# A feed-forward opening in a hybrid encoder layer: even and odd activations in shared buffers, a first product over one pair of token tiles, and an operand built inside the first unit

## The chip, the cores and the metric

The kernel runs on one core of a Trainium2 chip. The metric is the device time of one execution, in microseconds (us). Most of a kernel's time is its span, from the first to the last instruction. The engines are TensorE (PE, with its weight loads shown apart as PEld), VectorE (DVE), ScalarE (ACT), GpSimd (POOL) and SyncE (SP, which here issues nearly all DMAs). Instructions on one engine run in the order in which the program lists them; engines wait for each other by semaphores.

## The reference

One layer works on x of 1024 tokens by 1024 features, all in float32:

```
x = x + 1/2 * SwiGLU_1(RMSNorm(x))          # FFN 1
x = x + W_out [attention || HGRN2 both ways]  # mixer, one shared input projection
x = x + 1/2 * SwiGLU_2(RMSNorm(x))          # FFN 2
x = RMSNorm(x)

SwiGLU(h) = (silu(h @ w_gate) * (h @ w_up)) @ w_out      # hidden width 2816
```

The change lies in the first half of each SwiGLU, silu(h @ w_gate) * (h @ w_up). The mixer between the two is the same before and after.

## The kernel before

**Number format.** A float32 product is made of three passes in a faster format: each operand is split into a high part (a rounding cast on ACT, L103 or L185) and a low part (operand minus high part, a subtraction on DVE or POOL, L104 or L186). PE adds high x high, high x low and low x high into one PSUM bank. So each matmul of the algorithm is three instructions, and each operand must be cast and subtracted before use.

**Up projection (ffn_up).** The 1024 tokens lie in 8 tiles of 128. Four pairs (an even and an odd tile each, function pair, for FFN 1 pair1) are loaded; in FFN 1 each tile is normalised first: a square with sum on ACT (L121), nine small steps on DVE for 1/sqrt (rstd, L82 to L94), a scaling on DVE (L131). FFN 2 reads tiles that attention has already normalised and written to memory.

The activations form a 2 x 2 block matrix: B11 and B21 are the lower and upper 512 features of the even tiles, B12 and B22 those of the odd tiles. Function blocks(i) puts pair i into columns i*128 to i*128+127 of these four, each by h_op: four PE transposes into a PSUM bank (L182), a cast on ACT (L185), a subtraction on DVE (L186). The weights of one block f of 128 hidden columns form another 2 x 2: A11, A12 (gate, lower and upper features) and A21, A22 (up). There are 22 such blocks.

Blocks f = 0 and 1 are done plainly (function plain, L277: 8 block products; 96 matmuls of 256 columns for each half g of the columns). The other 20 are done by unit(f) with a scheme of seven block products in place of eight (L294, 12 matmuls of 512 columns each): A11 B11 and A12 B21, then S2 T2, A22 T4, S3 T3, S1 T1 and S4 B22. S1 to S4 are sums of weight blocks (made on POOL, L254 to L257), T1 to T4 sums of activation blocks, made by sums(i): t1 and t2 on DVE (L220, L222), t3 and t4 on POOL (L221, L223), and T2, T4 and T3 by h_op. T1 is put off: t1 is written to memory (L224), and last_sum reads it back (L230) and builds T1 when the buffer of B12, which only the plain blocks read, is free.

Each result goes through silu (ACT) and a product (DVE) and is written to act[f] in memory. Down projection and the rest follow later.

**Order of the opening.** blocks(0) and blocks(1); plain products of f = 0 and 1 over columns 0:256; sums and blocks of the others; plain products over 256:512; sums of pairs 2 and 3; last_sum four times; then the units, interleaved two by two:

```
for i in range(2):
    tiles[i] = blocks(i)
for f in range(early):
    A[f] = [weight_op(f, f"A{i}", src, early_lo) ...]
    plain(f, 0, A[f])
for i in range(2):
    sums(i, *tiles[i])
    tiles[i + 2] = blocks(i + 2)
for f in range(early):
    plain(f, 1, A[f])
```

This is the order of the program; a planner with a timeline of its own then fixes the order on each engine. Where several instructions are ready, the one that stands earlier in the program goes first.

**Buffers.** Pools hand out slots and make a new user wait until the old one has been read: B 4 slots (B11, B21, B12, B22, then T1 for B12), T 3, raw 7 (token tiles and raw weights), wop 9 (split weights, and the junk output of the squares), s 4 (t1 to t4, s1 to s4 and the reloaded t1), n 3 (snapshots p1, u2, u3 of PSUM), c 4 (results), PSUM 8 banks. The argument early_lo names the engine of the low parts of the plain blocks' weights: POOL in FFN 1, DVE in FFN 2.

Of the kernel before, what the change touches and what calls it, by code (L numbers as in the profile page):

```python
# [12 lines left out]
F32 = mybir.dt.float32  # L13
F32R = mybir.dt.float32r
# [3 lines left out]
ALU = mybir.AluOpType  # L18
# [3 lines left out]
P = 128  # L22
# [22 lines left out]
class Trunk:  # L45
# [142 lines left out]
    def ffn_up(self, name, pair, act, early_lo, mid):  # L188
# [75 lines left out]
        def result(what, nm):  # L264
            return self.cc.tile([P, 512], F32, name=f"{what}_{name}_{nm}", tag="c")

        def plain(f, g, A):

            cols = slice(g * 256, (g + 1) * 256)
            ps = [self.bank(f"pp{j}_{name}_{f}_{g}") for j in range(2)]  # L270
            for odd in ((0, 1) if g == 0 else (1, 0)):
                B = [op(key) for key in (("B12", "B22") if odd else ("B11", "B21"))]
                for j in range(2):
                    for k in range(NK):
                        ks = slice((k % 4) * P, (k % 4 + 1) * P)
                        for i, (a, b) in enumerate(((0, 0), (0, 1), (1, 0))):
                            nc.tensor.matmul(  # L277
                                ps[j][:, odd * 256 : (odd + 1) * 256],
                                A[2 * j + k // 4][:, a, ks], B[k // 4][:, b, k % 4, cols],
                                start=(k == 0 and i == 0), stop=(k == NK - 1 and i == 2),  # L280
                            )
            sg = result("sg", f"{f}_{g}")
            nc.scalar.activation(sg, ps[0], AF.Silu)
            nc.vector.tensor_mul(sg, sg, ps[1])
            nc.sync.dma_start(
                act[f].rearrange("p (h t) -> p h t", h=2)[:, :, cols],
                sg.rearrange("p (h t) -> p h t", h=2),
            )

        def product(ps, A, key, first):  # L290
            for k in range(4):
                ks = slice(k * P, (k + 1) * P)
                for i, (a, b) in enumerate(((0, 0), (0, 1), (1, 0))):
                    nc.tensor.matmul(  # L294
                        ps, A[:, a, ks], T[key][:, b, k, :],
# [4 lines left out]
        def unit(f):  # L300
# [43 lines left out]
        tiles = {}  # L344
        for i in range(2):
            tiles[i] = blocks(i)
        A = {}
        for f in range(early):
            A[f] = [weight_op(f, f"A{i}", src, early_lo) for i, src in enumerate(raw_weights(f))]
            plain(f, 0, A[f])  # L350
        for i in range(2):
            sums(i, *tiles[i])
            tiles[i + 2] = blocks(i + 2)
        for f in range(early):
# [623 lines left out]
def trunk_kernel(tc, io):  # L978
    nc = tc.nc
    with ExitStack() as ctx:  # L980
# [12 lines left out]
        def ffn(ctx, name, xn_pair, load, done, d_spec, opened, early_lo, mid=None, finish=None):  # L993
# [6 lines left out]
            with ExitStack() as up:  # L1000
                k.B, k.T = sbuf(up, "B", 4, side="right"), sbuf(up, "T", 3, side="right")
# [15 lines left out]
        with ExitStack() as c1:  # L1017
            gain = []

            def pair1(i):  # L1020
# [7 lines left out]
                for xt, t in zip(x, (2 * i, 2 * i + 1)):  # L1028
                    junk = k.wop.tile([P, D], F32R, name=f"junk_{t}", tag="wop").bitcast(F32)
                    k.norm_rows(xt, gain[0], xt, f"n0_{t}", junk=junk)  # L1030
# [125 lines left out]
```

## Time and profile before

| | us |
|---|---|
| three runs, median (lowest to highest) | 2119.46 (2116.44 to 2119.88) |
| the profiled execution | 2116.49 |
| its span | 2114.7 |
| FFN 1: first plain matmul, first matmul of the units | 29.97, 98.25 |
| FFN 2: first plain matmul, first matmul of the units | 1407.79, 1480.50 |

The profile is of one execution. A row of the timeline gives the start and length of one or more like instructions, the engine, the line of the code and the tiles; brackets hold the idle time before it and what ended it. A row of the windows gives, for one stretch of the span, how long each engine was busy. A busy PE is not always at its pace: waiting between pipelined matmuls is partly counted as busy, and the granted clock (PEclk, 1.00 is full) may be lower.

### The profile page before, as it was taken

How to read it: one execution, taken by the hardware profiler on the slowest of the kernel's cores; microseconds unless marked ns; L12 is line 12 of the kernel's file. 1: busy time of each engine (PE TensorE's matmuls, PEld its weight loads, DVE VectorE, ACT ScalarE, POOL GpSimd, SP SyncE). 2: the span in 40 equal slices, each digit the busy share in tenths (PEclk: the TensorE clock that was granted, in tenths of full speed). 3: DMA queues.
4: the chain of work that ended last, by engine and by line, in shares of the span. 5: the costliest groups of instructions: out<-in, count | busy, mean ns of one | idle time of the engine just before them, and what ended most of it. 6: DMA issues, size and time to landing. Idle time of an engine off the chain costs nothing.

```text
span 2114.7 us, 27958 instructions
## 1 busy us (share of the span) xinstructions
PE 2032.2 (96%) x10849; PEld 1754.3 (83%) x10849; DVE 1166.2 (55%) x1951; ACT 780.3 (37%) x1295; POOL 392.5 (19%) x278
## 2 busy tenths in 40 slices
PE   5899999999999899999999999988999999999998
PEld 5888888887888798989999788878888888878886
DVE  6565555545363506788872567753655555443634
ACT  4333333334343313333332546632433333333432
POOL 2333222310000000121120423311423222100000
PEclk9999999999999999999999999999999999999999
DMA  5422332127464211121234532263322221264542
GB/s 168 119 86 80 94 92 76 56 82 258 148 228 141 80 41 40 31 80 35 86 96 141 172 111 80 84 220 106 100 84 72 84 90 55 75 244 147 180 146 80
DMA packets 208124, 232.12 MB, mean 110 GB/s; under 512 B 9444, under 2 KB 169464, under 8 KB 207992
## 3 DMA queue, kind: packets, MB, share of 16 engines
q1 hardware_dynamic: 205688, 221.95, 33.3%
q0 software_dynamic: 2304, 8.39, 1.0%
q8 instruction: 85, 1.39, 0.3%
q14 instruction: 47, 0.39, 0.1%
HBM read 175.78 MB, written 54.53 MB: 109 GB/s over the span
## 4 chain that ended last, share of the span: by engine, by line
PE 90%; DVE 5%; DMA 2%; issue 1%; ACT 1%; POOL 0%; SPq 0%; DVEq 0%; ACTq 0%; POOLq 0%
PE py_ffn L402 22%; PE pa_ffn L294 15%; PE pd_ffn L294 10%; PE rec_ps L167 6%; PE pc_ffn L294 5%; PE pb_ffn L294 5%; PE pp_ffn L277 5%; PE ri_ps L495 2%; PE rg_ps L495 2%; PE py L855 2%; PE lv L561 2%; PE s L798 2%; PE pv L830 2%; PE pa L855 1%; PE aq_ps L495 1%
## 5 line engine op out<-in xcount | busy, mean ns | idle before, releaser
L402 PE MATMUL py_ffn<-hl_out_ffn,hl_act_ffn 128*128 128x512 f32 x2112 | 481.0, 390 | 4.5 <-ACT hl_out_ffn L103 3.4
L402 PEld LDWEIGHTS py_ffn<-hl_out_ffn,hl_act_ffn 128*128 128x128 f32 x2112 | 396.3, 188 | 88.4 <-ACT hl_out_ffn L103 4.9
L104 DVE TENSOR_TENSOR hl_out_ffn<-raw_out_ffn,hl_out_ffn 128x512 fp32r<-128x512 f32 x176 | 120.3, 689 | 233.9 <-ACT hl_out_ffn L103 233.8
L294 PE MATMUL pa_ffn<-ffn_T,hl_in_ffn_S 128*128 128x512 f32 x960 | 236.8, 390 | 0.0
L294 PEld LDWEIGHTS pa_ffn<-ffn_T,hl_in_ffn_S 128*128 128x128 f32 x960 | 180.4, 188 | 37.2
L103 ACT CAST hl_out_ffn<-raw_out_ffn 128x512 fp32r<-128x512 f32 x176 | 107.6, 619 | 265.1 <-PE py_ffn L402 248.6
L104 DVE TENSOR_TENSOR hl_in_ffn_S<-s_ffn,hl_in_ffn_S 128x512 fp32r<-128x512 f32 x160 | 167.3, 1050 | 25.4 <-ACT hl_in_ffn_S L103 22.0
L103 ACT CAST hl_in_ffn_S<-s_ffn 128x512 fp32r<-128x512 f32 x160 | 99.1, 621 | 192.0 <-PE pd_ffn L294 148.1
L104 DVE TENSOR_TENSOR hl_in_ffn_A<-raw_in_ffn,hl_in_ffn_A 128x512 fp32r<-128x512 f32 x128 | 106.7, 838 | 113.0 <-ACT hl_in_ffn_A L103 113.0
L103 ACT CAST hl_in_ffn_A<-raw_in_ffn 128x512 fp32r<-128x512 f32 x136 | 83.8, 624 | 174.9 <-PE pc_ffn L294 75.3
L167 PE MATMUL rec_ps<-hm,hl_rec_w 128*128 128x512 f32 x576 | 135.9, 395 | 0.0
L167 PEld LDWEIGHTS rec_ps<-hm,hl_rec_w 128*128 128x128 f32 x576 | 108.1, 190 | 21.8
L294 PE MATMUL pd_ffn<-ffn_T,hl_in_ffn_S 128*128 128x512 f32 x480 | 121.8, 389 | 0.0
L294 PE MATMUL pb_ffn<-ffn_B,hl_in_ffn_A 128*128 128x512 f32 x480 | 121.5, 390 | 0.0
L294 PE MATMUL pa_ffn<-ffn_B,hl_in_ffn_A 128*128 128x512 f32 x480 | 116.0, 391 | 0.0
L294 PE MATMUL pc_ffn<-ffn_T,hl_in_ffn_A 128*128 128x512 f32 x480 | 115.3, 390 | 0.0
L294 PE MATMUL pd_ffn<-ffn_B,hl_in_ffn_S 128*128 128x512 f32 x456 | 109.5, 390 | 0.0
L277 PE MATMUL pp_ffn<-ffn_B,hl_in_ffn_A 128*128 128x256 f32 x768 | 100.2, 293 | 6.6 <-ACT xn_n L121 2.2
L294 PEld LDWEIGHTS pa_ffn<-ffn_B,hl_in_ffn_A 128*128 128x128 f32 x480 | 90.4, 189 | 18.5
L294 PEld LDWEIGHTS pb_ffn<-ffn_B,hl_in_ffn_A 128*128 128x128 f32 x480 | 90.2, 188 | 18.6
L294 PEld LDWEIGHTS pc_ffn<-ffn_T,hl_in_ffn_A 128*128 128x128 f32 x480 | 90.2, 188 | 18.6
L294 PEld LDWEIGHTS pd_ffn<-ffn_T,hl_in_ffn_S 128*128 128x128 f32 x480 | 90.2, 188 | 18.6
(245 smaller groups left out, 3127.2 us busy)
## 6 DMA issues: line engine op xcount, KB each, us to landing
raw_in_ffn<-in_ffn_w_in SPq DMA_DIRECT2D x88, 512.0 KB, 4.1
raw_out_ffn<-in_ffn_w_out SPq DMA_DIRECT2D x88, 512.0 KB, 3.8
raw_act_ffn<-d_act SPq DMA_DIRECT2D x88, 256.0 KB, 4.0
d_act<-g_ffn SPq DMA_DIRECT2D x80, 256.0 KB, 2.2
x<-d_x SPq DMA_DIRECT2D x24, 512.0 KB, 4.9
x<-in_x SPq DMA_DIRECT2D x16, 512.0 KB, 5.1
d_x<-x SPq DMA_DIRECT2D x16, 512.0 KB, 2.8
raw_rec_w<-in_w_in_mix SPq DMA_DIRECT2D x12, 512.0 KB, 3.8
```

The source lines that it names most:

```text
L103: nc.scalar.copy(hl[:, 0, :], src)
L104: (lo_engine or nc.vector).tensor_sub(hl[:, 1, :], src, hl[:, 0, :].bitcast(F32))
L167: nc.tensor.matmul(out, hl[:, a, ks], h[half][b][:, k, cols], start=(k == 0 and i == 0), stop=(k == NK - 1 and i == 2),)
L277: nc.tensor.matmul(ps[j][:, odd * 256 : (odd + 1) * 256], A[2 * j + k // 4][:, a, ks], B[k // 4][:, b, k % 4, cols], start=(k == 0 and i = ...
L294: nc.tensor.matmul(ps, A[:, a, ks], T[key][:, b, k, :], start=(first and k == 0 and i == 0), stop=(k == 3 and i == 2), skip_group_check=True,)
L402: nc.tensor.matmul(py[d], ah[:, a, o : o + P], wo[d][:, b, :], start=(f == 0 and i == 0), stop=(f == NF - 1 and i == 2),)
L495: nc.tensor.matmul(ps[:, tt, :], h[half][a][:, k, ts], hl[k // 4][:, b, ws], start=(k == 0 and i == 0), stop=(k == NK - 1 and i == 2),)
L561: nc.tensor.matmul(pl[:, cs], now[:, 0, cs], now[:, 1, cs], start=True, stop=True)
L798: nc.tensor.matmul(ps[:, ks], qT[:, a, qs], kT[:, b, kv, ks], start=(i == 0), stop=(i == 2))
L830: nc.tensor.matmul(ps, vt[:, j, a, vs], pT[j][:, b, i4, :], start=(st == 0 and i == 0), stop=(st == NT - 1 and i == 2),)
L855: nc.tensor.matmul(py, lhs(a, n), units[n][:, b, ds], start=(n == 0 and i == 0), stop=(n == 3 and i == 2),)
```

## The change

Three things change, for both FFNs unless said otherwise.

1. B11 and B12 lie in one buffer, B21 and B22 in another (function both). plain takes a range of columns and reads even and odd tiles with one matmul, so its moving operand has two runs. T1 is written over B12 in place.
2. The order of the opening: block 0 over columns 0:128 after pair 0 alone; then pair 1 and block 1 over 0:256; then pairs 2 and 3 with the sums; then block 0 over 128:256 and 256:512 and block 1 over 256:512. t1 is loaded back, in the n and c pools, after the last sums, and T1 is built inside the first unit, behind its second product.
3. In FFN 1 the low parts of the plain weights are made on DVE; the squares share one junk buffer; the 1/sqrt of pairs 1 to 3 is done jointly for the two tiles (twelve steps on two columns), that of pair 0 tile by tile.

```diff
         def op(key):
+            if key[0] == "B" or key == "T1":
+                row, col = ("1", 1) if key == "T1" else (key[1], int(key[2]) - 1)
+                return both(row)[:, col]
             if key not in T:
-                pool = self.T if key in ("T2", "T3", "T4") else self.B
-                T[key] = pool.tile([P, 2, 4, 512], F32R, name=f"{name}_{key}", tag="T")
+                T[key] = self.T.tile([P, 2, 4, 512], F32R, name=f"{name}_{key}", tag="T")
+            return T[key]
+        def both(row):
+            key = f"B{row}"
+            if key not in T:
+                T[key] = self.B.tile([P, 2, 2, 4, 512], F32R, name=f"{name}_{key}", tag="B")
             return T[key]
...
-        def last_sum(i):
-            t1 = self.sums.tile([P, 512], F32, name=f"t1b_{name}_{i}", tag="s")
+        def load_sum(i):
+            pool, tag = (self.snap, "n") if i < 3 else (self.cc, "c")
+            t1 = pool.tile([P, 512], F32, name=f"t1b_{name}_{i}", tag=tag)
             nc.sync.dma_start(t1, t1s[i * P : (i + 1) * P, :])
-            self.h_op(op("T1"), t1, i, f"{name}_T1")
+            return t1
...
-        def plain(f, g, A):
-            cols = slice(g * 256, (g + 1) * 256)
+        def plain(f, A, lo, hi):
+            w = hi - lo
+            ps = [self.bank(f"pp{j}_{name}_{f}_{lo}") for j in range(2)]
+            halves = lambda t: t[:, : 2 * w].rearrange("p (h t) -> p h t", h=2)
+            B = [both(row) for row in "12"]
+            for j in range(2):
+                for k in range(NK):
+                    ks = slice((k % 4) * P, (k % 4 + 1) * P)
+                    for i, (a, b) in enumerate(((0, 0), (0, 1), (1, 0))):
+                        nc.tensor.matmul(
+                            halves(ps[j]), A[2 * j + k // 4][:, a, ks],
+                            B[k // 4][:, :, b, k % 4, lo:hi],
+                            start=(k == 0 and i == 0), stop=(k == NK - 1 and i == 2),
+                        )
...
             a = bank("pa")
             product(a, A["A11"], "B11", True)
-            p1 = snap("p1")
-            nc.scalar.copy(p1, a)
+            p1 = None
+            if f > early:
+                p1 = snap("p1")
+                nc.scalar.copy(p1, a)
             yield
             b = bank("pb")
             product(b, A["A12"], "B21", True)
+            if f == early:
+                for i in range(4):
+                    self.h_op(op("T1"), t1[i], i, f"{name}_T1")
+                p1 = snap("p1")
+                nc.scalar.copy(p1, a)
...
+        tiles[0] = blocks(0)
+        first(0)
+        plain(0, A[0], 0, 128)
+        tiles[1] = blocks(1)
+        first(1)
+        plain(1, A[1], 0, 256)
         for i in range(2):
+            tiles[i + 2] = blocks(i + 2)
             sums(i, *tiles[i])
-            tiles[i + 2] = blocks(i + 2)
-        for f in range(early):
-            plain(f, 1, A[f])
+        plain(0, A[0], 128, 256)
+        plain(0, A[0], 256, 512)
+        plain(1, A[1], 256, 512)
         for i in range(2, 4):
             sums(i, *tiles[i])
-        for i in range(4):
-            last_sum(i)
+        t1 = [load_sum(i) for i in range(4)]
...
-                k.B, k.T = sbuf(up, "B", 4, side="right"), sbuf(up, "T", 3, side="right")
+                k.B, k.T = sbuf(up, "B", 2, side="right"), sbuf(up, "T", 3, side="right")
...
+                ss = k.stat.tile([P, 2], F32, name=f"ss_n0_{i}", tag="ss2")
+                if not junk:
+                    junk.append(k.wop.tile([P, D], F32R, name="junk", tag="wop").bitcast(F32))
+                for j, xt in enumerate(x):
+                    nc.scalar.activation(junk[0], xt, AF.Square, accum_out=ss[:, j : j + 1])
+                joint = k.rstd(ss, 2, D, f"n0_{i}") if i else None
+                for j, xt in enumerate(x):
+                    r = joint[:, j : j + 1] if i else k.rstd(ss[:, j : j + 1], 1, D, f"n0_{j}")
+                    nc.vector.scalar_tensor_tensor(
+                        out=xt, in0=xt, scalar=r, in1=gain[0], op0=ALU.mult, op1=ALU.mult
+                    )
...
-            ffn(c1, "ffn1", ..., nc.gpsimd, lambda: k.vectors(k.raw), finish1)
+            ffn(c1, "ffn1", ..., nc.vector, lambda: k.vectors(k.raw), finish1)
```

The function first(f) loads and splits the four weight blocks of a plain block, as the loop over early did.

More of the change, by code (lines that the diff above doesn't have):

```diff
@@ L265, in result @@
             return self.cc.tile([P, 512], F32, name=f"{what}_{name}_{nm}", tag="c")
-        def plain(f, g, A):
-            cols = slice(g * 256, (g + 1) * 256)
[L270 to L284, printed above, removed]
+        def plain(f, A, lo, hi):
[12 more added lines that the diff above has]
+                        )
+            sg = result("sg", f"{f}_{lo}")
+            nc.scalar.activation(sg[:, : 2 * w], ps[0][:, : 2 * w], AF.Silu)
+            nc.vector.tensor_mul(sg[:, : 2 * w], sg[:, : 2 * w], ps[1][:, : 2 * w])
             nc.sync.dma_start(
-                act[f].rearrange("p (h t) -> p h t", h=2)[:, :, cols],
-                sg.rearrange("p (h t) -> p h t", h=2),
+                act[f].rearrange("p (h t) -> p h t", h=2)[:, :, lo:hi], halves(sg)
             )
@@ L1017, in trunk_kernel @@
         with ExitStack() as c1:
-            gain = []
+            gain, junk = [], []
             def pair1(i):
```

17 lines of the change are left out of this document (5 added, 12 removed).

## The prediction

> **What bounds the kernel now.** I read the page first: busy time of the engines over the span.
>
> ```profile
> span 2114.7 us, 27958 instructions
> PE 2032.2 (96%) x10849; PEld 1754.3 (83%) x10849; DVE 1166.2 (55%) x1951; ACT 780.3 (37%) x1295; POOL 392.5 (19%) x278
> ```
>
> TensorE (PE) sets the time almost everywhere, and time can only be won where PE is idle, or busy at less than its pace. The change touches one stage, the opening of each FFN, up to the first matmul of the seven-product units. Next I read the windows of that stage, for FFN 1 and then FFN 2 (length; busy us and instructions of PE, weight load, DVE, ACT, POOL; granted PE clock; DMA).
>
> ```profile
> core 0: us, PE busy (x) PEld busy (x) DVE busy (x) ACT busy (x) POOL busy (x), PEclk, DMA share, GB/s
> 0.00:9.39 9.39, 0.00 (x1) 0.03 (x1) 3.32 (x17) 3.58 (x5) 0.68 (x6) 1.00 0.81 271
> ...
> 9.39:29.97 20.58, 7.24 (x33) 6.36 (x33) 19.84 (x37) 11.72 (x21) 13.29 (x10) 1.00 0.70 208
> 53.20:65.58 12.38, 10.41 (x70) 7.84 (x69) 11.98 (x19) 8.02 (x15) 6.42 (x5) 0.95 0.66 196
> 89.20:98.25 9.05, 4.99 (x34) 4.58 (x33) 4.55 (x7) 3.69 (x7) 2.48 (x2) 0.83 0.51 145
> ...
> 1405.60:1410.74 5.14, 1.13 (x4) 0.56 (x4) 5.14 (x10) 3.75 (x9) 2.20 (x1) 0.85 1.02 304
> 1435.84:1448.20 12.36, 10.43 (x71) 7.83 (x69) 11.91 (x19) 8.02 (x15) 6.30 (x5) 0.94 0.66 197
> 1471.73:1480.50 8.77, 4.98 (x34) 4.57 (x33) 4.56 (x7) 3.69 (x7) 2.48 (x2) 0.83 0.47 149
> ```
>
> The row from 9.39 shows the first plain matmul waiting for DVE, which is busy 19.84 of 20.58 us. In the middle ones PE does little more than 56 transposes while DVE is full (11.98 of 12.38). The last ones are a hole at the seam to the units. The PE timeline says what ended each hole (start, us, engine, line; in brackets the idle time and what ended it).
>
> ```profile
> 26.64 3.67 PE L182 MATMUL pt_ffn_B<-ident,x 128*128 128x128 f32 x16 [12.49 <-DVE x L131]
> 29.97 23.41 PE L277 MATMUL pp_ffn<-ffn_B,hl_in_ffn_A 128*128 128x256 f32 x192
> ...
> 92.76 0.63 PE L182 MATMUL pt_ffn_T<-ident,t1b_ffn 128*128 128x128 f32 x4 [1.63 <-DMA t1b_ffn<-d_t_ffn]
> 95.81 2.79 PE L182 MATMUL pt_ffn_T<-ident,t1b_ffn 128*128 128x128 f32 x12 [2.42 <-DMA t1b_ffn<-d_t_ffn]
> 98.25 3.14 PE L294 MATMUL pa_ffn<-ffn_B,hl_in_ffn_A 128*128 128x512 f32 x12
> 101.23 2.88 PE L294 MATMUL pb_ffn<-ffn_B,hl_in_ffn_A 128*128 128x512 f32 x12
> 103.95 2.88 PE L294 MATMUL pc_ffn<-ffn_T,hl_in_ffn_A 128*128 128x512 f32 x12
> ...
> 1402.28 3.27 PE L182 MATMUL pt_ffn_B<-ident,xn 128*128 128x128 f32 x28 [0.89 <-DVE x L899]
> 1407.79 0.89 PE L277 MATMUL pp_ffn<-ffn_B,hl_in_ffn_A 128*128 128x256 f32 x2 [2.23 <-ACT xn_n L121]
> 1410.74 25.26 PE L277 MATMUL pp_ffn<-ffn_B,hl_in_ffn_A 128*128 128x256 f32 x189 [1.46 <-ACT hl_in_ffn_A L103]
> 1480.50 3.16 PE L294 MATMUL pa_ffn<-ffn_B,hl_in_ffn_A 128*128 128x512 f32 x12
> ```
>
> So the first plain product begins at 29.97 in FFN 1, because the second pair of token tiles was normalised late, and FFN 2's stream runs from 1410.74. The units begin at 98.25 and 1480.50, after a wait for T1's reload. My paces: a 256-column matmul 23.41/192 = 122 ns, a 512-column one (103.95 - 101.23)/12 = 227 ns, a transpose 3.27/28 = 117 ns.
>
> Why was DVE so late in FFN 1? The DVE and POOL timelines, first DVE without POOL, then beside it:
>
> ```profile
> 6.29 0.22 DVE L88 SCALAR_TENSOR_TENSOR rs_n<-rs_n 128x1 f32<-128x1 f32 x1
> 9.39 1.06 ACT L121 ACTIVATE junk<-x 128x1024 f32<-128x1024 f32 x1 [2.40 <-DMA x<-in_x]
> 17.50 1.86 DVE L88 SCALAR_TENSOR_TENSOR rs_n<-rs_n 128x1 f32<-128x1 f32 x2
> 18.08 7.43 POOL L104 TENSOR_TENSOR hl_in_ffn_A<-raw_in_ffn,hl_in_ffn_A 128x512 fp32r<-128x512 f32 x6
> 24.23 2.36 DVE L131 SCALAR_TENSOR_TENSOR x<-x,rs_n,g_ffn_norm 128x1024 f32<-128x1024 f32 x1
> 26.95 1.28 DVE L131 SCALAR_TENSOR_TENSOR x<-x,rs_n,g_ffn_norm 128x1024 f32<-128x1024 f32 x1
> ```
>
> A one-column step of 0.22 us comes out at 0.9 us, and a row scaling of 1.28 us at 2.36 us, while POOL makes the weights' low parts. DVE is held up by POOL.
>
> **The change, part by part.** *Plain matmuls.* Per FFN 384 of 256 columns (46.8 us) become 96 of 256 and 144 of 512: 11.7 + 32.7 = 44.4 us, 2.4 us less. Each now reads its moving operand in two runs, an even and an odd one, a whole block apart; no row shows that form. Below nothing I exclude, since the columns streamed are the same; above, I bound it by a second pass (122 and 227 ns more). I take nothing, after the nearest rows: the units' 512-column matmuls from 101.23 on keep 227 ns whatever operand pair they read. The Trainium skill, SBUF — State Buffer (Door 1: The DMA port swizzle, its remark on cachelines), says that accesses within a 16-byte line run at full bandwidth and that one which crosses to a new line pays; by it two long unbroken runs would cost no more than one, and the sum stays. No run here shows it.
>
> *Low parts on DVE in FFN 1.* POOL loses 8 subtractions, DVE gets 8, and the contention of 14 to 25 us goes. FFN 2 had them on DVE already.
>
> ```profile
> L186 DVE TENSOR_TENSOR ffn_B<-pt_ffn_B,ffn_B 128x512 fp32r<-128x512 f32 x32 | 20.6, 679 | 0.0
> L104 POOL TENSOR_TENSOR hl_in_ffn_A<-raw_in_ffn,hl_in_ffn_A 128x512 fp32r<-128x512 f32 x8 | 10.4, 1324 | 0.0
> L92 DVE TENSOR_TENSOR rs_ao<-rs_ao 128x2 f32<-128x2 f32 x12 | 2.5, 209 | 0.3
> ```
>
> *FFN 1, start.* The load of tiles 2 and 3 is now issued behind two weight loads on SP; tile 2, which ACT now waits for until 9.39, comes about 3.9 us later, an estimate: 1 MB at the 271 GB/s of the first window. That is before DVE is through with pair 0. Tile 1's scaling no longer stands behind tile 2's sum. DVE has, from 5.7 us on, for pair 0: two chains of nine steps at about 0.2 us (3.8), two scalings (2.6), four low parts of B and four of A at 20.6/32 = 0.65 (5.2). The first half of these eight lets PE start at about 14; all are there by 5.7 + 11.6 = 17.3. So PE starts 16 us earlier, with 5.9 us of work.
>
> *FFN 1, to the upper columns.* The product over columns 256:512 needs all four pairs. DVE's list until then: 3.8 + three joint chains of twelve steps (7.2) for the rstd, eight scalings 10.2, 16 low parts of B 10.4, eight of A 5.2, four subtractions for t1, t2 at 0.68 (2.7), six low parts of T 3.9, one silu product 0.7: 44.1 us, so 49.8 at best. PE's own list until then is shorter: 14 + 5.9 + 10.9 + 5.9 and 72 transposes (8.4) = 45.1. DVE is what is late next. I add 3 us for POOL's t3 and t4 and for in-order waits: 53. Then PE alone: 96 matmuls 21.8, 24 transposes 2.8. Units at 77.6 instead of 98.25: 20.6 us.
>
> *The seam.* The operands S of a unit take these durations:
>
> ```profile
> L104 DVE TENSOR_TENSOR hl_in_ffn_S<-s_ffn,hl_in_ffn_S 128x512 fp32r<-128x512 f32 x160 | 167.3, 1050 | 25.4 <-ACT hl_in_ffn_S L103 22.0
> L103 ACT CAST hl_in_ffn_S<-s_ffn 128x512 fp32r<-128x512 f32 x160 | 99.1, 621 | 192.0 <-PE pd_ffn L294 148.1
> L254 POOL TENSOR_TENSOR s_ffn<-raw_in_ffn 128x512 f32<-128x512 f32 x40 | 53.0, 1326 | 252.5 <-DVE hl_in_ffn_S L104 201.5 <-PE pt_ffn_T L182 47.1 <-issue 3.8
> ```
>
> The T1 loads go ahead of the last plain products, behind the write of t1, in buffers of their own (n and c in place of s). On SP, weight loads and act writes queue behind them; 21.8 us of matmuls cover that. If not, 4 us of hole return. The holes of 1.63 and 2.42 us are in the 20.6 already. T1's 16 transposes return inside the unit: +1.9 us. The p1 copy on ACT now stands behind T1's four casts, and the sum g0 and the next product into bank pa stand behind p1; the product A22 T4 (2.7 us) covers it. s1 to s4 on POOL get their buffers later relative to the unit's start than now, and DVE also has T1's low parts: I put 1 us of starving in the first unit (between 0 and the 4.3 us that s1, s2, a cast and a subtraction take together: 2 x 1.33 + 0.62 + 1.05). FFN 1 net: 20.6 - 1.9 - 1.0 = 17.7.
>
> *FFN 2.* Tokens come normalised. Pair 0 alone needs 16 transposes, to about 1403.7; ACT and DVE then have eight casts and eight low parts, and the first half gives a start at about 1405.5. PE work after it: 44.4 + 96 transposes 11.2 = 55.6, so 1461.1. In the middle 12.36 us held 56 transposes (6.6 us) and four matmuls (0.5): about 5 us were lost to DVE. Now the product over 128:256 (5.9 us), ready long before, fills them. I add 2 us for seams and 1.7 us for the clock:
>
> ```profile
> 1410.74:1413.00 2.26, 2.26 (x10) 2.26 (x11) 2.26 (x5) 1.75 (x2) 0.00 (x0) 0.50 1.02 405
> 1413.00:1415.00 2.00, 2.00 (x12) 2.00 (x11) 1.79 (x9) 0.00 (x0) 0.00 (x0) 0.50 0.33 126
> 1417.00:1419.00 2.00, 2.00 (x19) 2.00 (x18) 0.00 (x0) 0.00 (x0) 0.47 (x1) 1.00 0.47 195
> ```
>
> After the hole, 22 matmuls took 4.26 us, against 2.7 at 122 ns. Units at 1464.8 instead of 1480.5: 15.7, less 1.9 and 1.0: 12.8. The last tile, 7, is loaded from 1419.90 on:
>
> ```profile
> 1419.90 0.32 SPq L1088 DMA_DIRECT2D xn<-d_xn  x1
> ```
>
> Its pair's turn on PE comes after 1405.5 + 5.9 + 10.9 + 5.9 = 1428, so it is hidden.
>
> One junk buffer for all squares costs nothing: ACT runs them in order anyway.
>
> **Sum.** 17.7 + 12.8 = 30.5 us off the profiled execution of 2116.49 (span 2114.7): 2086.0. That execution lies at the low end of the runs (2116.44 to 2119.88, median 2119.46), so I add 1 us: **2087**.
>
> **Rivals.**
> *A, the overlap does not come.* A read over both halves may be taken as touching what lies between them, or the planned order may put the copies of pair 1 and the 128:256 product late. Then PE waits about 4 us between the first two products, and the middle 5 us per FFN stay: 18 of the 30.5 gone, 2105. For it: in the middle windows PE got only four matmuls between the transposes. Against: there nothing else was ready.
> *B, the clock.* Each new wait (for pair 1, for the upper columns) may cost half clock again, about 1.7 us each, four times: 2094. The trace is unclear: FFN 1's first 192 matmuls run at 122 ns after a hole of 12.49 us, with 16 transposes between (229 ns each, twice the 117 ns). The Trainium skill, TensorE: Matmul & The Clock Gate (Part 1, the clock gate), says that an idle window of about 3.4 us halves the clock until one as long is busy; the rows at 1410 agree in kind.
> *C, slower.* The two-run moving operand costs time on every one of the 480 matmuls. It decides from 30.5/480 = 64 ns each; at a second pass it is 88.8 us, less 30.5: about 2175. Only that the form is not in the trace speaks for it.
> *D, no change.* The change doesn't do what it says: in the planned order the first product still stands behind the other pairs, and starving eats the seam. Then only the 4.8 us of shorter matmuls are left, less the 2 us in the units: 2117.5 - 2.8, about 2115.
>
> **How the numbers follow.** About 0.2% (4.2 us) is what can be told from no change. Forecast (2078 to 2097) 0.55, B 0.09, A 0.20, D 0.05, C 0.07, and 0.04 for lists that pack without seams: the 3 + 2 + 2 + 1.7 us that I added fall away, and a little more, under 2078. The range 2074 to 2107 holds the forecast, B and most of A. Faster 0.88, within 0.05, slower 0.07.
>
> **What would show it.** PE's first plain matmul near 14 and near 1405; L104 of A on DVE at about 0.65 us, and no 1.8 us one-column steps; 512-column plain matmuls at 227 ns; plain matmuls among the transposes; no wait for t1b; the units' first matmul at about 78 us in FFN 1, and in FFN 2 about 16 us sooner after the last matmul of attention than now. Wrong if: the plain matmuls' pace is over 180 or 290 ns, PE still waits over 8 us in all between 14 and 77, or the first unit takes over 3 us longer than its 84 matmuls and 16 transposes (19.1 + 1.9).

## The result, and the profile after

On the same chip the changed kernel took 2098.70 us (median of 4 runs, 2096.25 to 2102.02) against 2117.95 us before (4 runs, 2115.84 to 2119.88): a ratio of 0.991, 95% interval 0.9889 to 0.9931. That is 19.2 us faster, where 32 were forecast (2087 against the 2119.46 known then). The number of the forecast, 2087, is missed by 12 us; the range, 2074 to 2107, holds the time. The profiled execution took 2101.0 us. First the page of after, busy time of the engines over the span:

```profile
span 2099.2 us, 27330 instructions
PE 2025.4 (96%) x10561; PEld 1734.2 (83%) x10561; DVE 1138.1 (54%) x1943; ACT 779.7 (37%) x1297; POOL 381.4 (18%) x270
```

PE lost 288 matmuls and only 6.8 us of busy time, while the span lost 15.5: more than half of the gain is idle time of PE. To see where, I cut both spans at the same instructions. A stage ends where the first matmul of the next begins; the mixer here runs from the first `rec_ps` matmul to the end of attention's last output matmul.

| stage (us) | before | after | measured | forecast |
|---|---|---|---|---|
| FFN 1, to the first matmul of the units | 98.25 | 84.14 | -14.1 | -20.6 |
| FFN 1, units | 383.32 | 386.14 | +2.8 | +2.9 |
| FFN 1, down projection, norm, first mixer product | 303.78 | 306.05 | +2.3 | 0 |
| mixer | 615.61 | 620.29 | +4.7 | 0 |
| FFN 2, to the first matmul of the units | 79.54 | 64.01 | -15.5 | -15.7 |
| FFN 2, units | 382.95 | 385.91 | +3.0 | +2.9 |
| FFN 2, down projection, end | 251.26 | 252.68 | +1.4 | 0 |
| span | 2114.7 | 2099.2 | -15.5 | -30.5 |

Of the 15.0 us that are missing, 6.5 are in FFN 1's opening, 8.4 in three stages whose code the change does not touch, 0.1 elsewhere.

**FFN 1's opening.** The PE timeline of after (start, us, engine, line, operation, count; in brackets the idle time before it and what ended it):

```profile
14.62 1.97 PE L182 MATMUL pt_ffn_B<-ident,x 128*128 128x128 f32 x8 [3.39 <-DVE x L1056]
17.42 0.80 PE L287 MATMUL pp_ffn<-ffn_B,hl_in_ffn_A 128*128 128x256 f32 x2 [0.83 <-ACT ffn_B L185]
19.59 8.29 PE L287 MATMUL pp_ffn<-ffn_B,hl_in_ffn_A 128*128 128x256 f32 x46 [1.37 <-DVE ffn_B L186]
...
31.32 0.73 PE L287 MATMUL pp_ffn<-ffn_B,hl_in_ffn_A 128*128 128x512 f32 x2 [1.70 <-ACT ffn_B L185]
32.66 12.06 PE L287 MATMUL pp_ffn<-ffn_B,hl_in_ffn_A 128*128 128x512 f32 x46 [0.61 <-DVE ffn_B L186]
...
51.23 27.78 PE L287 MATMUL pp_ffn<-ffn_B,hl_in_ffn_A 128*128 128x256 f32 x144
...
81.47 0.66 PE L182 MATMUL pt_ffn_T<-ident,t_ffn 128*128 128x128 f32 x4 [1.15 <-DVE t_ffn L231]
82.89 1.60 PE L182 MATMUL pt_ffn_T<-ident,t_ffn 128*128 128x128 f32 x8 [0.76 <-POOL t_ffn L232]
84.14 4.19 PE L303 MATMUL pa_ffn<-ffn_B,hl_in_ffn_A 128*128 128x512 f32 x12
...
90.88 1.91 PE L182 MATMUL pt_ffn_T<-ident,t1b_ffn 128*128 128x128 f32 x16
```

The product over one pair begins at 17.42, not 29.97, and the T1 transposes stand in the first unit (90.88) without a wait. But the first product is full of small losses: 46 matmuls took 8.29 us, 180 ns each (before: 122), and the second product's 46 took 12.06, 262 ns each instead of 227. After 32.66 PE has no hole to speak of until 81.5: the 56 transposes from 44.56 to 51.23 lie close together, and the 144 matmuls from 51.23 are the 48 over 128:256 and the 96 over 256:512 in one go. The windows of after say what DVE did in the second product, with the granted clock (length; busy us and count of PE, weight load, DVE, ACT, POOL; PEclk; DMA):

```profile
19.59:27.88 8.29, 8.29 (x48) 8.29 (x49) 5.69 (x18) 5.38 (x10) 0.48 (x1) 1.00 0.86 294
32.66:44.56 11.90, 11.90 (x46) 9.69 (x47) 6.34 (x14) 0.60 (x1) 0.00 (x0) 0.88 0.15 55
```

DVE is busy in 6.34 of 11.90 us there: PE is the bound, not DVE. The slower pace is the clock. The trace keeps the granted clock as records of a start, a length and a share; it has 0.50 from 32.12 to 35.54 us, where the matmuls start 427 ns apart, and 1.00 behind it, where they start 227 ns apart. Why the start is at 17.42 rather than 14 shows in the ACT and DVE timelines of after:

```profile
9.58 1.14 ACT L103 CAST hl_in_ffn_A<-raw_in_ffn 128x512 fp32r<-128x512 f32 x2 [2.59 <-DMA raw_in_ffn<-in_ffn_w_in]
10.23 0.69 DVE L104 TENSOR_TENSOR hl_in_ffn_A<-raw_in_ffn,hl_in_ffn_A 128x512 fp32r<-128x512 f32 x1 [0.77 <-ACT hl_in_ffn_A L103]
13.28 1.28 DVE L1056 SCALAR_TENSOR_TENSOR x<-x,rs_n,g_ffn_norm 128x1024 f32<-128x1024 f32 x1
...
16.79 1.07 ACT L185 CAST ffn_B<-pt_ffn_B 128x512 fp32r<-128x512 f32 x2
...
23.85 1.06 ACT L1052 ACTIVATE junk<-x 128x1024 f32<-128x1024 f32 x1 [2.44 <-DMA x<-in_x]
25.04 0.17 DVE L82 TENSOR_SCALAR rs_n<-ss_n 128x2 f32<-128x2 f32 x1 [2.39 <-ACT junk L1052]
...
25.53 2.48 DVE L1056 SCALAR_TENSOR_TENSOR x<-x,rs_n,g_ffn_norm 128x1024 f32<-128x1024 f32 x2
```

The planned order puts low parts of the weights (10.23) ahead of tile 1's scaling (13.28) on DVE; they wait for ACT's cast, and that waits 2.59 us for the weights' DMA. The 1.86 us pairs of one-column steps are gone. The scaling of pair 1 (25.53) is late for another reason. The first step of pair 2's 1/sqrt (25.04) stands inside pair 1's chain of steps on DVE; it waits 2.39 us for ACT's sum, and ACT waits 2.44 us for that tile's load. So the second product, which needs pair 1, waits for the load of pair 2.

**FFN 2's opening**, PE timeline of after:

```profile
1400.92 0.51 PE L287 MATMUL pp_ffn<-ffn_B,hl_in_ffn_A 128*128 128x256 f32 x2 [1.44 <-ACT ffn_B L185]
1404.56 16.69 PE L287 MATMUL pp_ffn<-ffn_B,hl_in_ffn_A 128*128 128x256 f32 x94
1428.14 27.79 PE L287 MATMUL pp_ffn<-ffn_B,hl_in_ffn_A 128*128 128x256 f32 x144
1460.64 3.01 PE L303 MATMUL pa_ffn<-ffn_B,hl_in_ffn_A 128*128 128x512 f32 x12
```

94 matmuls (46 of 256 and 48 of 512 columns) in 16.69 us, where 122 and 227 ns give 16.5: here the pace is full from the start.

**The stages in between.** Windows of the recurrence and attention's last output matmuls, before:

```profile
869.98:1038.97 168.99, 166.59 (x1151) 154.66 (x1150) 140.90 (x242) 59.08 (x70) 40.04 (x14) 0.99 0.22 66
...
1389.92:1400.96 11.04, 11.04 (x51) 9.09 (x51) 6.38 (x25) 1.66 (x3) 1.88 (x2) 1.00 0.79 248
```

and after:

```profile
860.96:1031.93 170.97, 166.54 (x1151) 153.38 (x1150) 147.32 (x241) 58.93 (x70) 40.83 (x14) 1.00 0.21 66
...
1384.07:1396.63 12.56, 12.56 (x51) 10.21 (x51) 6.39 (x25) 1.66 (x3) 1.88 (x2) 0.87 0.67 230
```

The recurrence has the same PE work (166.6 us) but 4.43 us of idle PE instead of 2.40, and 6.4 us more of busy DVE. The output matmuls have no idle time at all and a granted clock of 0.87 instead of 1.00: 1.5 us of clock. The remaining 1.2 us of the mixer lie mainly in its attention part between these two windows. In the recurrence the clock hides part of the difference: the trace of before has 0.50 there from 914.31 to 917.72 us, that of after has none. The recurrence of run 4 below, which has before's order between the FFNs, and no such stretch either:

```profile
869.46:1037.10 167.64, 165.23 (x1151) 153.23 (x1150) 140.94 (x241) 58.97 (x70) 40.07 (x14) 1.00 0.22 67
```

At the same clock the difference is thus 3.3 us. The seam from the down projection to the mixer, PE timeline of before, then of after:

```profile
738.37 11.27 PE L495 MATMUL ri_ps<-hl_ri_w,hm 128*128 128x256 f32 x85
```

```profile
728.85 11.65 PE L515 MATMUL ri_ps<-hl_ri_w,hm 128*128 128x256 f32 x84 [1.40 <-DVE hm L151]
```

A wait of 1.40 us is new there. Code that nobody touched runs in another order: by a count that leaves buffer numbers out, 281 of the 5000 PE instructions between the two FFNs stand elsewhere in the planned list.

### The profile page after: what moved, and what is told of

The parts are those of the page before. It is cut to its first block, busy times and chain, and to the rows that moved or that the text cites. A ratio compares the mean times of both kernels' runs of the same rounds, so it can differ in the third digit from the quotient of the medians.

```text
span 2099.2 us, 27330 instructions
## 1 busy us (share of the span) xinstructions
PE 2025.4 (96%) x10561; PEld 1734.2 (83%) x10561; DVE 1138.1 (54%) x1943; ACT 779.7 (37%) x1297; POOL 381.4 (18%) x270
## 4 chain that ended last, share of the span: by engine, by line
PE 88%; DVE 6%; DMA 2%; ACT 2%; issue 2%; POOL 1%; SPq 0%; DVEq 0%; POOLq 0%; ACTq 0%
PE py_ffn L422 22%; PE pa_ffn L303 15%; PE pd_ffn L303 10%; PE rec_ps L167 5%; PE pc_ffn L303 5%; PE pb_ffn L303 5%; PE pp_ffn L287 4%; PE ri_ps L515 2%; PE rg_ps L515 2%; PE py L875 2%; PE s L818 2%; PE pa L875 2%; PE lv L581 2%; PE pv L850 2%; PE av_ps L515 1%
## 5 line engine op out<-in xcount | busy, mean ns | idle before, releaser
L303 PE MATMUL pd_ffn<-ffn_B,hl_in_ffn_S 128*128 128x512 f32 x936 | 226.4, 389 | 0.6 <-DVE ffn_B L186 0.6
L303 PEld LDWEIGHTS pa_ffn<-ffn_T,hl_in_ffn_S 128*128 128x128 f32 x960 | 180.2, 188 | 37.4
L303 PEld LDWEIGHTS pd_ffn<-ffn_B,hl_in_ffn_S 128*128 128x128 f32 x936 | 175.6, 188 | 37.5 <-DVE ffn_B L186 1.0
L104 DVE TENSOR_TENSOR hl_in_ffn_S<-s_ffn,hl_in_ffn_S 128x512 fp32r<-128x512 f32 x160 | 145.8, 916 | 61.9 <-ACT hl_in_ffn_S L103 61.9
L104 DVE TENSOR_TENSOR hl_in_ffn_A<-raw_in_ffn,hl_in_ffn_A 128x512 fp32r<-128x512 f32 x136 | 99.5, 738 | 118.5 <-ACT hl_in_ffn_A L103 118.4
L303 PE MATMUL pb_ffn<-ffn_B,hl_in_ffn_A 128*128 128x512 f32 x480 | 115.3, 389 | 0.0
L303 PEld LDWEIGHTS pa_ffn<-ffn_B,hl_in_ffn_A 128*128 128x128 f32 x480 | 90.8, 190 | 19.4 <-DVE ffn_B L186 0.6
L287 PE MATMUL pp_ffn<-ffn_B,hl_in_ffn_A 128*128 128x512 f32 (+1 forms) x480 | 94.6, 360 | 6.0 <-ACT ffn_B L185 4.0
L265 POOL TENSOR_TENSOR s_ffn<-s_ffn,raw_in_ffn 128x512 f32<-128x512 f32 x40 | 64.0, 1599 | 200.1 <-issue 197.2
```

Source lines behind the costliest of these rows:

```text
L104: (lo_engine or nc.vector).tensor_sub(hl[:, 1, :], src, hl[:, 0, :].bitcast(F32))
L265: nc.gpsimd.tensor_sub(s2, s1, a11)
L287: nc.tensor.matmul(halves(ps[j]), A[2 * j + k // 4][:, a, ks], B[k // 4][:, :, b, k % 4, lo:hi], start=(k == 0 and i == 0), stop=(k == NK ...
L303: nc.tensor.matmul(ps, A[:, a, ks], op(key)[:, b, k, :], start=(first and k == 0 and i == 0), stop=(k == 3 and i == 2), skip_group_check=True,
```

## The experiments

Two theories about the missing time were to be told apart. **O**: the planner, with other times at the opening, orders the untouched stages otherwise, and that order is slower. **S**: those stages differ by chance from one execution to the next, and only the openings count. Two more concern FFN 1's start and come with their runs. Ratios are to the kernel before on the same chip, with 95% intervals.

**1 and 2: both kernels again.** No edit.

> The changed kernel, unchanged, profiled and timed once more. In the first profile the two openings gained 14.1 and 15.5 us up to the units and the units gave back 2.8 and 3.0, which makes 23.8; yet the median moved only 19.2, and the profiled span 15.5. The missing time lies in stages whose code is not touched: first down projection 303.8 to 306.1 us, mixer with attention 615.6 to 620.3, second down projection 240.7 to 241.8. Theory O (the planner's order): 281 of the 5000 PE rows between the two FFNs stand at other places than before, and this order is slower; then mixer and attention take 619 to 621 us again, while the down projections, whose order is the same, come back to 303 to 305. Theory S (scatter between executions): mixer and attention come out anywhere from 614 to 621. Median 2096 to 2102 either way.

> The kernel before, profiled once more. Theory O: mixer and attention 615 to 617 us again. Theory S: they can come out at 620 as well, as the first down projection may come out at 306. Median 2116 to 2120, ratio 1.

After: 2099.02 us, 0.9922 (0.9909 to 0.9936). Before: 2115.72 us, 0.9996 (0.9987 to 1.0005). In the profiles, after's stages came back within 0.5 us (mixer 620.63, first down projection 306.17, FFN 1 opening 83.75), before's within 0.6 (615.88, 303.80, 98.81). The executions that were profiled are alike, which speaks against chance for the 4.7 and 2.3 us. O had put the mixer at 619 to 621 us again, and that came; it had also put the first down projection back at 303 to 305, and that did not. The other runs do spread, by 5 to 7 us here.

**3 and 4: the change in one FFN only.** The other FFN keeps the old ffn_up.

```diff
+NEW = ("ffn1",)     # 3;  ("ffn2",) in 4
```

> The change in FFN 1 alone; FFN 2 runs its old opening. The middle has the planned order of the changed kernel. Local sum: FFN 1 gains 14.1 - 2.8 = 11.3 us. Theory O: 4 to 5 of them are given back in mixer and attention (619 to 621 us), so 2111 to 2113 (6 to 7 us faster). Theory S: 2106 to 2108 (11 us faster), mixer and attention near 616.

> The change in FFN 2 alone; FFN 1 and the middle are planned as before, row by row on PE. The opening gains 15.5 and the units give back 3: 12.5 us, 2105 to 2107, under both theories, with mixer and attention at 615 to 617 under theory O. If it gains 16 or more, or under 9, the sum by stages is wrong.

FFN 1 alone: 2108.06 us, 0.9966 (0.9956 to 0.9976), 8.2 us better. FFN 2 alone: 2104.92 us, 0.9942 (0.9929 to 0.9956), 11.3 better. Together 19.5; the whole change gained 19.2, and 17.2 on this chip (run 1): the two add up, or nearly. FFN 2 alone has the planned order of before between the FFNs, and its mixer takes 615.94. FFN 1 alone has after's order and a mixer of 622.50; but its profiled run was its slowest (2112.47), and by its median it sits where S put it, so this pair does not decide.

**5: T1's part alone.** Before, with load_sum, T1 inside the first unit and p1 behind it; nothing else.

```diff
-        for i in range(4):
-            last_sum(i)
+        t1 = [load_sum(i) for i in range(4)]
...
+            if f == early:
+                for i in range(4):
+                    self.h_op(op("T1"), t1[i], i, f"{name}_T1")
```

> The kernel before with T1's part alone: t1 reloaded early into the n and c buffers, T1 built inside the first unit. The planned order between the FFNs is that of the changed kernel (2 of 5000 PE rows differ from it, 279 from before). By stages: each opening ends 6.5 to 7 us earlier (the waits of 1.6 and 2.4 us, 16 transposes, and their slow pace go), each FFN's units take 2.5 to 3 us more, together 7 to 8.5 us. Theory O (the middle's planned order costs time, by its place in the program and not by chance): mixer and attention 619 to 623 us and first down projection near 306, so only 0 to 2 us in all, 2114 to 2116. Against it (the middle does not matter): 2108 to 2109.

2116.01 us, 0.9998 (0.999 to 1.0007): nothing. By its profile the openings are 7.5 us (90.78) and 6.7 us (72.84) shorter, as meant, but the units are 3.9 us longer each, the first down projection 2.4 and the mixer 3.7 (619.29). 14.2 gained, 13.8 given back: 7.7 by the transposes and waits of the unit, 6.1 in stages that it does not touch (2.7 of them in the output matmuls, which take 13.69 us at a granted clock of 0.80).

**6: two runs per matmul alone.** Before, with shared buffers and plain over columns lo to hi; the order of the opening stays.

```diff
-                                A[2 * j + k // 4][:, a, ks], B[k // 4][:, b, k % 4, cols],
+                            halves(ps[j]), A[2 * j + k // 4][:, a, ks],
+                            B[k // 4][:, :, b, k % 4, lo:hi],
```

> The kernel before with the shared buffers alone: even and odd columns in one 512-column matmul, old order, old T1, low parts on POOL as before. The 192 matmuls of 512 columns with two runs show their pace: 227 ns if the form is free, up to 454 if each run is a pass. If free, each opening is 2.4 us shorter or, as the same columns wait for the same operands, a little less: 4 to 5 us together. The middle is planned as in the changed kernel: theory O adds 5 to 8 us and makes it 2116 to 2120, no faster than before. Against it: 2111 to 2112.

2113.43 us, 0.9981 (0.9972 to 0.9991), between the two forecasts. The openings are 4.5 and 6.0 us shorter (93.78, 73.59), the units 1.0 and 1.5 longer, the mixer 3.4. PE timeline of this run:

```profile
33.72 21.56 PE L286 MATMUL pp_ffn<-ffn_B,hl_in_ffn_A 128*128 128x512 f32 x92
```

92 matmuls with two-run operands at 234 ns, next to 227 in the units; the first of them, until 34.7 us, run at half pace.

Experiments 5 and 6 together shorten FFN 1's opening by 12.0 us. The whole change shortens it by 14.1. By that difference, if the parts add, the early start, which brings PE's first product 12.5 us forward, was worth only some 2 us there (its parts were not run without the other two).

**7 and 8: is it the clock?** After, with 8 or 16 transposes of tile 0 ahead of FFN 1's first product, into a bank that nobody reads.

```diff
+        if name == "ffn1":
+            warm = self.bank("warm")
+            for i in range(16):          # 8 in 7
+                ks = slice(i % 4 * P, (i % 4 + 1) * P)
+                nc.tensor.transpose(warm[:, ks], tiles[0][0][:, ks], self.ident)
```

> The changed kernel with 8 idle transposes of tile 0 on PE ahead of FFN 1's first product; the middle is planned as in the changed kernel (2 of 5000 PE rows differ). First product as before at 180 ns a matmul or a little faster. Theory O: mixer and attention 619 to 623, median 2097 to 2100.

> The same with 16 idle transposes, in which the planner puts the middle back into the order of the kernel before (2 of 5000 PE rows differ from it). Theory O: mixer and attention 615.5 to 616.5, so 4 to 7 us faster than with 8: 2091 to 2095. If the order does not matter: within 2 us of the kernel with 8. The second reading is the clock: if half clock in the first product (46 matmuls in 8.29 us) comes from idle PE before it, it falls towards 5.6 us.

PE timeline with 16:

```profile
16.20 2.41 PE L370 MATMUL warm<-ident,x 128*128 128x128 f32 x16
18.37 0.48 PE L287 MATMUL pp_ffn<-ffn_B,hl_in_ffn_A 128*128 128x256 f32 x2
19.41 5.78 PE L287 MATMUL pp_ffn<-ffn_B,hl_in_ffn_A 128*128 128x256 f32 x46 [0.56 <-DVE ffn_B L186]
...
31.07 12.26 PE L287 MATMUL pp_ffn<-ffn_B,hl_in_ffn_A 128*128 128x512 f32 x46 [0.57 <-DVE ffn_B L186]
```

and with 8:

```profile
19.46 5.77 PE L287 MATMUL pp_ffn<-ffn_B,hl_in_ffn_A 128*128 128x256 f32 x46 [0.87 <-DVE ffn_B L186]
...
30.84 10.72 PE L287 MATMUL pp_ffn<-ffn_B,hl_in_ffn_A 128*128 128x512 f32 x46 [0.70 <-DVE ffn_B L186]
```

The transposes stand where PE had waited, the first product's 46 start at the same time as in after (19.4 and 19.5 against 19.59) and take 5.8 us instead of 8.29. With 8 the pace had been expected to stay near 180 ns. The times are 2094.49 us, 0.9898 (0.9884 to 0.9912), with 8 and 2092.27 us, 0.9887 (0.9872 to 0.9903), with 16, the fastest of this study; the changed kernel stood at 0.991 and 0.9922, each against the kernel before on its own chip. The two intervals overlap, so these times do not decide between O and S. The opening falls to 80.59 with 8 and 82.60 with 16. The second product is a separate matter: 233 ns with 8, 267 with 16, at granted clocks of 1.00 and 0.87. The kernel with 16 also has the planned order of before between the FFNs; its first down projection takes 303.61 as before, its mixer 618.05, half of the way back; the rest lies in the output matmuls (13.78 us at a granted clock of 0.79, where before had 11.04 at 1.00).

**9 and 10: is it the weights' low parts on DVE?** After, where in FFN 1 the low parts of block 0's weights multiply by a one that is made from tile 1's 1/sqrt, so that they cannot be put ahead of it. 10 adds the 16 transposes.

```diff
+                nc.vector.scalar_tensor_tensor(
+                    out=hl[:, 1, :], in0=src, scalar=self.one[0], in1=hl[:, 0, :].bitcast(F32),
+                    op0=ALU.mult, op1=ALU.subtract,
+                )
...
+                        nc.vector.tensor_scalar(k.one[0], r, 0.0, 1.0, ALU.mult, ALU.add)
```

> The changed kernel, but the low parts of the first block's weights in the first FFN multiply by a one that is made from tile 1's 1/sqrt, so that the DVE scales tile 1 ahead of them. Theory W (the first product starts late because DVE waits in order for the weights' DMA ahead of tile 1's scaling): the scaling starts at 10 to 11 us instead of 13.28, the first 46 matmuls in a row begin at 16 to 17.5 instead of 19.59, and the first unit at 81 to 82 instead of 84.14. Rival (it starts late for the weights themselves, which the first product needs anyway): the scaling moves, the 46 matmuls do not, and the first unit stays at 83.5 to 84.5. Between the FFNs the planner gives this kernel almost the order of before (68 of 5000 PE rows stand elsewhere, 351 against the changed kernel), so theory O (order) adds 4 to 6 us less there: 2090 to 2094 with W, 2093 to 2096 without it; with W and no effect of the order 2096 to 2098.

> The kernel of the run before with 16 transposes of tile 0 ahead of the first product, whose result nobody reads. With the row that 16 such transposes gave in the changed kernel (46 matmuls in 5.78 us instead of 8.29), the first product gains up to 2.5 us and the transposes take up to 1.8 of it unless PE waits there anyway: the first unit at 79 to 81, the time 1 to 2.5 us under the run before. If the half clock costs nothing once the start is early, the time stays within 0.5 us of it or gets longer by 1.

DVE and PE timelines of 9:

```profile
10.00 1.28 DVE L1063 SCALAR_TENSOR_TENSOR x<-x,rs_n,g_ffn_norm 128x1024 f32<-128x1024 f32 x1
...
14.90 0.80 PE L294 MATMUL pp_ffn<-ffn_B,hl_in_ffn_A 128*128 128x256 f32 x2 [1.59 <-ACT ffn_B L185]
18.14 8.35 PE L294 MATMUL pp_ffn<-ffn_B,hl_in_ffn_A 128*128 128x256 f32 x46 [2.45 <-DVE ffn_B L186]
25.73 0.17 DVE L82 TENSOR_SCALAR rs_n<-ss_n 128x2 f32<-128x2 f32 x1 [2.41 <-ACT junk L1059]
27.77 1.10 PE L182 MATMUL pt_ffn_B<-ident,x 128*128 128x128 f32 x8 [1.28 <-DVE x L1063]
...
33.54 12.31 PE L294 MATMUL pp_ffn<-ffn_B,hl_in_ffn_A 128*128 128x512 f32 x46 [0.96 <-DVE ffn_B L186]
```

The scaling moves from 13.28 to 10.00 and the first two matmuls from 17.42 to 14.90, as theory W said. Then the gain melts: the 46 move by 1.45 us, the second product comes 0.9 us later (33.54 against 32.66), the units begin at 84.86. W is right about the start and wrong about what it is worth. The second product needs pair 1, and pair 1's transposes wait for its scaling on DVE (27.77). Ahead of that scaling stands, as in after, the first step of pair 2's 1/sqrt (25.73), which waits 2.41 us for ACT's sum. PE timeline of 10:

```profile
18.04 5.77 PE L294 MATMUL pp_ffn<-ffn_B,hl_in_ffn_A 128*128 128x256 f32 x46 [2.63 <-DVE ffn_B L186]
28.70 3.68 PE L182 MATMUL pt_ffn_B<-ident,x 128*128 128x128 f32 x16 [4.90 <-DVE x L1068]
```

With the first product over at 23.8, PE waits 4.90 us for pair 1's scaling; the units begin at 83.35, not at the 79 to 81 expected. The totals, 2096.58 us, 0.9901 (0.9884 to 0.9919), and 2098.03 us, 0.9905 (0.989 to 0.9921), do not tell the two apart; the second was to be 1 to 2.5 us shorter.

**11: the order, as cleanly as it can be had.** 24 transposes instead of 16. The planned order between the FFNs flips back to after's (2 of 5000 elsewhere).

> The changed kernel with 24 idle transposes instead of 16: the same edit with 8 more of them, but the planner gives the stages between the FFNs the order of the changed kernel again (2 of 5000 PE rows elsewhere, 279 against before). Theory O (that order costs time): 2 to 6 us slower than with 16, 2095 to 2098, with the first down projection and the mixer together 3 us or more longer. Rival (the order is worth nothing, what differed were the openings): only the 8 transposes, at most 1 us, so 2092 to 2093.5.

2094.80 us, 0.9891 (0.9874 to 0.9908): the interval overlaps that of 16. Down projection and mixer together take 2.35 us more (304.07 + 619.94 against 303.61 + 618.05), under the 3 that O asked for. Where the order bites is plain, though. The recurrence with 16, then with 24:

```profile
857.18:1026.09 168.91, 166.54 (x1151) 154.64 (x1150) 141.34 (x241) 59.12 (x70) 40.08 (x14) 0.99 0.21 66
```

```profile
857.55:1028.18 170.63, 166.53 (x1151) 153.39 (x1150) 146.96 (x241) 58.92 (x70) 40.83 (x14) 1.00 0.21 66
```

The first has 3.4 us at 0.50 in it (from 901.27), the second none: here too the clock hides part of the difference.

**12: low parts on POOL again.**

```diff
-            ffn(c1, "ffn1", ..., nc.vector, ...)
+            ffn(c1, "ffn1", ..., nc.gpsimd, ...)
```

> The changed kernel with the low parts of the plain weights in FFN 1 made on POOL again, as before the change; the order between the FFNs stays that of the changed kernel (2 of 5000 PE rows elsewhere). Theory P (POOL holds DVE up, as the 1.86 us pair of one-column steps and the 2.36 us scaling beside POOL's subtractions in the kernel before say): steps of 0.2 us at 0.6 us and more beside POOL's subtractions again, the second product later than 31.3, the first unit at 87 to 92 instead of 84.14, the time 2102 to 2107. Rival (DVE is in order behind the weights' DMA, so taking eight subtractions of 0.65 us and their waits off it frees as much as contention costs): the first unit at 82 to 85, the time within 2 us of the changed kernel's 2099.

2100.52 us, 0.9929 (0.9911 to 0.9947), the same as the changed kernel, as the rival had it. DVE, POOL and PE timelines of this run:

```profile
12.35 0.69 DVE L186 TENSOR_TENSOR ffn_B<-pt_ffn_B,ffn_B 128x512 fp32r<-128x512 f32 x1 [1.08 <-ACT ffn_B L185]
12.96 1.22 DVE L229 TENSOR_TENSOR t_ffn<-x,x 128x512 f32<-128x512 f32 x1
...
18.29 1.21 DVE L83 TENSOR_SCALAR rs_n<-rs_n 128x2 int32<-128x2 int32 x1
...
10.14 5.18 POOL L104 TENSOR_TENSOR hl_in_ffn_A<-raw_in_ffn,hl_in_ffn_A 128x512 fp32r<-128x512 f32 x3 [8.84 <-ACT hl_in_ffn_A L103]
...
19.43 5.04 POOL L104 TENSOR_TENSOR hl_in_ffn_A<-raw_in_ffn,hl_in_ffn_A 128x512 fp32r<-128x512 f32 x4
...
16.52 7.84 PE L287 MATMUL pp_ffn<-ffn_B,hl_in_ffn_A 128*128 128x256 f32 x46 [0.82 <-DVE ffn_B L186]
...
82.52 3.01 PE L303 MATMUL pa_ffn<-ffn_B,hl_in_ffn_A 128*128 128x512 f32 x12
```

The contention is real (the two-column step at 18.29, 0.16 us elsewhere, takes 1.21 beside POOL's t4, which runs from 18.19 to 19.47), yet the opening is no longer, 82.52. DVE has lost 8 subtractions and their waits, which is worth as much.

## Why the prediction was right, and where it was off

**Right.** *Two runs cost nothing.* In after 144 matmuls took 27.78 us; 48 x 122 + 96 x 227 ns give 27.6. Rival C is out, and the rule cited there from the Trainium skill, SBUF — State Buffer (Door 1: The DMA port swizzle), agrees. *The seam.* No wait for t1b, and units longer by 2.8 and 3.0 us where 2.9 were put. In FFN 1 that is partly luck: the 1 us put for starving does not show as idle PE (1.71 us in the units before and after), while the first 12 matmuls took 4.19 us at a granted clock of 0.69, against 3.14 at 0.96. *FFN 2's opening:* -15.5 against -15.7. Its 3.7 us for seams and clock came as 3.7 us of idle PE between 1400.92 and 1460.64, at a granted clock of 1.00; that waits took the place of the 1.7 put for the clock is luck too. *The wrong-if bounds* on waits and the first unit were not passed. The one on the pace, 180 ns, was just reached in the first product (8.29 us / 46 = 180.2 ns), through the half pace at its start and not through the two runs.

**Mis-sized: FFN 1's opening, 14.1 in place of 20.6.** The step that failed is "DVE is what is late next". It set the upper columns at 53, by DVE's list plus 3, and hid PE's list, 45.1, behind it with 7.9 us to spare. In the run PE ended its list later than DVE: at 51.23 all 72 transposes were done and the product over 128:256 was still to come, so the list ended at 57.1. Against 45.1 the trace of after shows +3.4 for the start at 17.42 instead of 14; +4.6 in the first product (17.42 to 27.88 instead of 5.9), of which 2.7 are the pace of 180 ns; +1.5 ahead of the second (27.88 to 31.32, with 1.9 of transposes), where pair 1 waits for the load of pair 2; +2.3 in the second (31.32 to 44.56 instead of 10.9), of which 1.6 are the clock of 0.88. That is 11.8; less the 7.9 to spare it leaves 3.9. The last transposes add 2.3: they waited for DVE's and POOL's last t (79.01 to 84.14 instead of 2.8). Together 6.2 of the 6.5 us. Rival A's late product over 128:256 came true, and did not matter: after 32.66 PE had no hole to fill. Rival B, the clock, came true in FFN 1, for which the sum had no clock term: 2.7 us in the first product, 1.6 in the second and 1.0 in the first matmuls of the units, 5.3 of the four times 1.7 that it had put.

Runs 7 and 8 show the pace to be one of PE's warming up, and worth 2.5 us. Runs 9 and 10 show that the late start is not worth its 3.4 us, because the second product hangs on pair 1. Run 12 shows that moving the low parts off POOL, which the prediction counted as relief ("DVE is held up by POOL"), is worth nothing that can be measured, though the contention itself was read rightly.

**A term left out: the stages between, +8.4 us.** The sum took for granted that code which is not edited keeps its time. Its planned order, its buffers and its clock changed.

*Order, in the recurrence.* All eight profiles with after's order have 3.9 to 4.5 us of idle PE there and take 170.6 to 172 us; all six with before's order, or nearly (68 of 5000 elsewhere in 9 and 10), have 2.4 and take 167.6 to 169. Without a stretch of half clock it is 167.6 (4, 9) against 170.6 to 171.0 (after, 1, 3, 5, 6, 11, 12), with one 168.9 to 169.0 (before, 2, 8, 10) against 171.9 (7). So O holds for **2 us** of the pair compared here, and for 3 at like clock.

*Clock, in the output matmuls.* They take 11.0 to 13.8 us under either order, at a granted clock of 0.79 to 1.00.

*A buffer, in the first down projection with its seam.* It is long (305.5 to 307.0 us) in after, 1, 3, 5, 9, 10 and 12, and short (303.6 to 304.2) in before, 2, 4, 6, 7, 8 and 11, which is neither grouping. The programs as built tell them apart. The mixer's first product, ri_ps, takes PSUM banks 0 and 1 in every kernel. In all seven long ones one of the last two banks that the transposes ahead of it write (pt_n, which DVE has to read for hm first) is bank 0 or 1; in none of the seven short ones is that so, and PE's list in this stage has the same order in before as in after. So the new wait of 1.40 us (0.74 in 10, where it is the last bank but one) comes from the bank that the planner chose, which neither O nor S had thought of. The other 0.9 us are busy PE: this stage has 13.7 us at 0.50 in after and 10.2 in before.

*Clock, in the second down projection.* The nine profiles that take 252.3 to 252.7 us there have 3.4 us at 0.50 that begin 0.6 to 1.8 us into the stage; the five that take 251.2 to 251.6 have none. What brings this stretch on was not tried.

S is right about part of it: runs of one kernel spread by up to 13 us (before, on the chip of run 12: 2110.15 at a mean granted clock of 0.991, 2123.05 at 0.983), so a single profile's stage carries some us of clock.

## What to carry to other kernels

Where a planner fixes the order and the buffers, an edit's sum has a term for every stage after it: cut both profiles at the same instructions, compare the stages that the edit does not name, and compare them at the same clock. Work that starts earlier with half its data is worth what the next wait leaves of it: follow the second product's inputs, not only the first's, and list the engines' work side by side with the true start and pace before one is called the bound. An idle gap ahead of a first product can carry matmuls that nobody reads, and these can pay.

## What the runs showed of the hardware

*PE starts at half pace, and the printed clock does not show it.* In after's first product matmuls start 213 ns apart until 25.3 us and 120 ns from then on, with a printed clock of 1.00 in all of the window 19.59:27.88. The trace's first clock record begins at 25.30; what lies ahead of it has no record and is printed as 1.00. In all fourteen traces the first record and the change of pace fall together, with 8 idle transposes at 19.1 us, with 16 at 17.2. So ahead of the first record the mean time of a matmul tells the pace, and the column does not. Behind it the column holds: 427 ns apart at 0.50, 227 at 1.00. The rule of the Trainium skill, TensorE: Matmul & The Clock Gate (Part 1), that PE is at half pace until it has been busy for a window of about 3.4 us, fits in kind: with 16 idle transposes PE works nearly without a hole from 14.44 us and is at full pace from 17.2; in after dense work from 19.59 became fast after 5.7 us.

*Not everything on DVE suffers beside POOL.* In run 12, while POOL is at its subtractions (10.14 to 24.5), a 128x512 subtraction on DVE that reads one operand from PSUM (L186) keeps its 0.69 us. One that reads both from SBUF (L229) takes 1.22 us instead of 0.68, and a two-column step 1.21 instead of 0.16.
